# Issuing 88 small stores from ScalarE behind its own copies, in a block of attention, delta-net and feed-forward layer

## The chip, the core and the metric

The kernel runs on one core of a Trainium2 chip. The metric is the device time of one execution in microseconds (us). The engines of the core are named as in its profile: PE (matrix multiplication, with PEld for its weight loads), DVE (vector), ACT (scalar and activation functions, "ScalarE"), POOL (general) and SP (synchronisation; here it does nothing but issue DMAs). Each engine works through its own instruction stream in order; an instruction starts when the semaphores it waits for are set. A DMA is issued by an instruction in one engine's stream and then moves on its own.

## The reference

One transformer block for a sequence of 1024 positions of width 1024, in float32:

```
mod = silu(c) @ w_ada + b_ada                       # six modulation vectors
h   = rmsnorm(x) * (1 + sc1) + sh1
q_a,k_a,v_a, q_d,k_d,v_d,z_d, b_d,a_d = split(h @ w_in)
y_attn  = dilated_attention(q_a, k_a, v_a)          # 8 heads of 64, three dilated branches, bias
y_delta = gated_deltanet(q_d, k_d, v_d, z_d, b_d, a_d)
          # conv + silu, l2norm, chunked delta rule with a triangular solve per chunk
          # and a scan over the chunks, rmsnorm * silu(z)
x = x + g1 * (concat(y_attn, y_delta) @ w_out)
h = rmsnorm(x) * (1 + sc2) + sh2
x = x + g2 * ((silu(h @ w_gate) * (h @ w_up)) @ w_down)
return rmsnorm(x)
```

## The kernel before, in words

Every matrix product of full precision is made of three products of reduced-precision parts: an operand is split into a high part (a rounded copy, made by ACT at line 216) and a low part (the difference, made by POOL at line 217). `hh` and `hl` are the two parts of h, `wh_*` and `wl_*` those of a weight slab, `wr_*` the slab as it comes from memory (issued by SP at line 215).

The work runs in this order. First the modulation and the norm (to about 90 us) and the first projections; then the delta-net for head group 0 (convolutions, key products, the inverse of the triangular matrices on DVE, a scan over 8 blocks at about 268 to 312 us); the same for head group 1 (preparation at about 318 to 366 us, inverse at 373 to 402, scan at 441 to 476); the attention of 8 heads (from about 478 to 700 us); then the output projection and the feed-forward layer, which take the rest.

The delta-net and the attention are chains that go from engine to engine, and PE would stand still in them. So the remaining projections are laid into these waits as filling. A generator (`others()`, with the modulation's products mixed in by `mixed()`) hands out projection matmuls one small piece at a time in this order: z0, kd, qd, vd of group 1, z1, then for each of four head pairs the attention values va (two slabs) and the keys and queries a_4, a_0. A table `FILL` names a point of the chain (for instance `S0_0_0`, `trv3_0`, `sb0_6`) and the amount of filling to put ahead of it; `turn(name)` applies it, `ahead` draws the pieces, `hold` and `until` make sure that a projection is done before its reader needs it. Within these bounds the final order on each engine is decided by the scheduler of the framework, from dependencies, buffers, priorities (`urgent()` raises one) and its own model of durations. The issuing engine of a DMA is part of what that scheduler weighs.

A projection gathers in one of two PSUM banks ("g banks"). When it is done, an evacuating function copies it out of the bank on ACT:

- `va_evac(c)` (line 1056 on): copies 128x256 of attention values into a tile `va` (line 1061) and stores it into `va_d` (line 1062).
- `spill(name, dst)` (line 1065 on): copies a 128x512 bank in two halves into tiles `sp_*` (line 1070) and stores each (line 1071) into `pj_d` (delta-net: kd, qd, vd of group 1) or `qk_d` (attention keys and queries).
- `z_evac(g)` (line 611 on) does the same for z with a SiLU on ACT, a product on POOL and a store on SP; it is not touched.

The tiles `va` and `sp_*` share one tag `vt` with two buffers, so the third copy waits until the first store has landed.

In the delta scan (`delta_scan`), each of 8 steps has `state(n)`: PE products into a bank `st`, DVE makes R, PE multiplies by U (line 974), ACT copies VN out in two halves (line 978), PE multiplies VN into the new state (line 982), DVE adds it up. `readout(n-1)` makes the output o of the step before (ACT copy at line 1016), and `flip(n-3)` turns the output of three steps before by PE transposes (line 1038), copies it out on ACT (`yt`, line 1042, one buffer) and stores it in `yd_d` (line 1043).

Readers of the stored data: `fetch` (line 1151, xp from `pj_d`), `att_load` (lines 1209 and 1217, va and raw from `va_d` and `qk_d`; ACT then scales the raw queries to QS at line 1223 and rounds the raw keys to KS at line 1228, POOL makes the difference KL at line 1229, and the scores S of lines 1254 and 1255 use them), and the output projection, which reads `yd_d` at line 1355.

Before the change all 964 DMAs of the program are issued by SP, on one queue, in SP's order.

Of the kernel before, what the change touches and what calls it, by code (L numbers as in the profile page):

```python
# [23 lines left out]
HALF = 512  # L24
# [46 lines left out]
def build(tc, I, out):  # L71
    nc = tc.nc
# [20 lines left out]
    def urgent():  # L93
        return tc.high_priority(offset=6000)
# [42 lines left out]
    def sbank(name):  # L137
        return psb(name, "s", 2)
# [416 lines left out]
    @contextmanager  # L555
    def turn(name):

        with tc.issue_after(last[0].ins) if ahead(FILL.get(name, 0)) else ExitStack():
            yield
# [388 lines left out]
    def delta_scan(g, st):  # L948
# [84 lines left out]
        def flip(n, o):  # L1033
            tk = slice(n * P, (n + 1) * P)
            ps = sbank(f"yt{g}_{n}")
            with turn(f"sy{g}_{n}"):
                for q in range(2):
                    nc.tensor.transpose(
                        ps[:, q * P : (q + 1) * P], o[:, 2 * q : 2 * q + 2, :].rearrange("p h d -> p (h d)"), ident
                    )  # L1040
            yt = pd.tile([P, 2, P], F32, name=f"yt{g}_{n}", tag="yt", bufs=1)
            nc.scalar.copy(yt.rearrange("p q t -> p (q t)"), ps[:, 0:256])
            nc.sync.dma_start(_.yd[g][:, :, tk].rearrange("q p t -> p q t"), yt)

        kept, outs = {}, {}
        for n in range(8 + 3):
            if n < 8:
                state(n)
            if 1 <= n <= 8:
                outs[n - 1] = readout(n - 1, *kept.pop(n - 1))  # L1050
            if n >= 3:
                flip(n - 3, outs.pop(n - 3))
# [4 lines left out]
    def va_evac(c):  # L1057
        def f(tb, ps):
            t = pv.tile([P, 256], F32, name=f"va{c}_{tb}", tag="vt", bufs=2)
            with urgent():  # L1060
                nc.scalar.copy(t, ps[:, 0:256])
            nc.sync.dma_start(_.va[c][tb], t)
        return f

    def spill(name, dst):
        def f(hf, ps):
            for i in range(2):
                t = pv.tile([P, 256], F32, name=f"sp_{name}_{hf}_{i}", tag="vt", bufs=2)
                with urgent():
                    nc.scalar.copy(t, ps[:, 256 * i : 256 * i + 256])  # L1070
                nc.sync.dma_start(dst[:, HALF * hf + 256 * i : HALF * hf + 256 * i + 256], t)
        return f

    def va_end(c):
# [388 lines left out]
    for hf in range(2):  # L1463
# [4 lines left out]
        for d in range(KT):  # L1468
            slabs = [(wsplit(I["wo"][d, 0], 512, f"wo{d}_0_{hf}"), 0)]
            t = x2[d, hf]  # L1470
# [206 lines left out]
    for k in range(4):  # L1677
# [3 lines left out]
        t = px.tile([P, HALF], F32, name=f"t2_{k}", tag="m", bufs=5)  # L1681
# [232 lines left out]
```

## Time and profile before

| | |
|---|---|
| time, median of three runs | 1443.23 us (1440.9 to 1454.74) |
| profiled execution | 1445.04 us, its span 1443.3 us |
| mean granted PE clock | 0.985 |
| PE busy | 95% of the span |
| ACT, DVE, POOL busy | 46%, 61%, 21% |
| DMA queue, share of 16 engines | 54.4%, 244 MB |
| the moved stores | 88 of 128 KB each, between 177 and 610 us |

The span is the stretch from the first to the last instruction that the profiler recorded; the profiled execution's own time lies 1.7 us above it. Busy time of an engine leaves out what it spends waiting and issuing DMAs. A row of waits gives who waited (engine, tile, line), for whom, the total in us, how many times and the longest. A row of a timeline gives the start, the duration, the engine, the line, the operation and its tiles; in square brackets stands the idle time just before it and what ended it. "SPq" is SP issuing a DMA: its duration is that of the issue, not of the transfer.

### The profile page before, as it was taken

Reading aid. Unit: us, or ns where it says so; the run is one execution under the profiler, and the core shown is the slowest. Engines: PE = TensorE matmul, PEld = TensorE weight load, DVE = VectorE, ACT = ScalarE, POOL = GpSimd, SP = SyncE. Lnnn points to the kernel's source line nnn. Section 1 sums busy time; section 2 is a strip of 40 time slices with the busy share of each in tenths; the row PEclk is TensorE's granted clock in tenths of the full one; section 3 lists DMA queues with packets and bytes.
Section 4 is the critical chain, followed back from the end, with each engine's and each line's share of the span. In section 5 each row is a group of like instructions: output and inputs, shape, how many; then the busy total and the mean of one; then the engine's idle time right before and its main releaser. Section 6 shows DMA issues by size and latency. Waiting matters only on the chain.

```text
span 1443.3 us, 24528 instructions
## 1 busy us (share of the span) xinstructions
PE 1372.5 (95%) x8984; PEld 1112.9 (77%) x8984; DVE 875.8 (61%) x1660; ACT 668.3 (46%) x1283; POOL 310.3 (21%) x279
## 2 busy tenths in 40 slices
PE   7998989997999699999998989999999999999997
PEld 4776857787879677777876868888888888888885
DVE  3587762665746223376426997757576776474487
ACT  3487523348233345576337743333333333444456
POOL 1345412243333334454244300000000000000000
PEclk9998999999999999999999999999999999999999
DMA  8736464466541643651375445636354565766666
GB/s 300 244 119 172 139 197 148 148 183 185 156 121 45 190 109 103 187 147 67 127 229 163 147 137 177 204 108 211 124 182 144 163 217 183 265 213 202 194 222 234
DMA packets 171921, 245.69 MB, mean 170 GB/s; under 512 B 33078, under 2 KB 76391, under 8 KB 171800
## 3 DMA queue, kind: packets, MB, share of 16 engines
q1 hardware_dynamic: 171800, 244.12, 54.4%
q8 instruction: 71, 1.16, 0.4%
q14 instruction: 50, 0.41, 0.1%
HBM read 181.30 MB, written 67.48 MB: 172 GB/s over the span
## 4 chain that ended last, share of the span: by engine, by line
PE 58%; DVE 6%; DMA 4%; ACT 2%; issue 1%; POOL 1%; SPq 0%; DVEq 0%; ACTq 0%; POOLq 0%
PE wua L1536 8%; PE wga L1536 8%; PE X L1731 6%; PE g_a L570 5%; PE wuc L1536 4%; PE Z L1731 4%; PE wgc L1536 4%; PE wo L570 3%; PE y L1295 2%; PE Y L1731 2%; PE tr L1278 2%; PE wgb L1536 2%; PE wub L1536 2%; PE g_va L593 2%; PE S L1254 1%
## 5 line engine op out<-in xcount | busy, mean ns | idle before, releaser
L1526 DVE TENSOR_TENSOR wl_db<-wr_db,wh_db 128x512 fp32r<-128x512 f32 x77 | 53.2, 691 | 76.4 <-ACT wh_db L1525 76.2
L1525 ACT CAST wh_db<-wr_db 128x512 fp32r<-128x512 f32 x77 | 47.9, 622 | 98.7 <-PE X L1731 41.3
L1258 DVE CUSTOM_DVE_ANT_0 X<-S,ng 128x512 f32<-128x512 f32 (+3 forms) x64 | 36.7, 587 | 71.5 <-PE S L1255 58.4
L1263 ACT ACTIVATE X<-X,sc 128x128 f32<-128x128 f32 (+7 forms) x64 | 49.4, 773 | 42.0 <-DVE sc L1258 36.6
L1731 PE MATMUL X<-wl_db,wh_da 128*128 128x512 f32 x176 | 68.6, 390 | 0.2 <-DVE wl_db L1526 0.2
L1731 PE MATMUL X<-wh_db,wh_da 128*128 128x512 f32 x176 | 68.6, 390 | 0.0
L1731 PE MATMUL X<-wh_db,wl_da 128*128 128x512 f32 x176 | 68.5, 389 | 0.0
L1265 POOL TENSOR_SCALAR X<-X,sc 128x128 f32<-128x128 f32 (+7 forms) x64 | 49.9, 782 | 82.3 <-DVE sc L1264 80.8
L1526 DVE TENSOR_TENSOR wl_da<-wr_da,wh_da 128x512 fp32r<-128x512 f32 x77 | 52.7, 686 | 1.2 <-ACT wh_da L1525 1.2
L570 PE MATMUL g_a<-hh,wh_a 128*128 128x512 f32 x128 | 53.2, 416 | 0.0
L570 PE MATMUL wo<-yh,wh_wo 128*128 128x512 f32 x128 | 51.5, 404 | 1.0 <-DVE xo L1346 1.0
L570 PE MATMUL wo<-yl,wh_wo 128*128 128x512 f32 x128 | 50.5, 394 | 0.9 <-DVE yl L1357 0.9
L570 PE MATMUL g_a<-hl,wh_a 128*128 128x512 f32 x128 | 51.0, 398 | 0.0
L570 PE MATMUL g_a<-hh,wl_a 128*128 128x512 f32 x128 | 50.7, 396 | 0.0
L570 PE MATMUL wo<-yh,wl_wo 128*128 128x512 f32 x128 | 50.6, 396 | 0.0
L1525 ACT CAST wh_da<-wr_da 128x512 fp32r<-128x512 f32 x77 | 47.3, 616 | 5.8 <-PE wua L1536 5.8
L1525 ACT CAST wh_wg_s<-wg_s 128x512 fp32r<-128x512 f32 x33 | 20.5, 622 | 55.4 <-PE wuc L1536 23.5
L1278 PE MATMUL tr<-ident,X 128*128 128x128 f32 x288 | 43.3, 277 | 2.8 <-DVE et L1281 1.8
L1254 PE MATMUL S<-KS,QS 128*128 128x512 f32 (+3 forms) x96 | 35.7, 380 | 10.2 <-ACT KS L1228 8.0
L217 POOL TENSOR_TENSOR wl_wo<-wr_wo,wh_wo 128x512 fp32r<-128x512 f32 x24 | 33.1, 1382 | 56.9 <-ACT wh_wo L216 55.9
L1295 PE MATMUL y<-et,va 128*64 128x128 f32 x576 | 42.8, 279 | 0.0
L1278 PEld LDWEIGHTS tr<-ident,X 128*128 128x128 f32 x288 | 33.0, 140 | 11.9 <-issue 4.6
(545 smaller groups left out, 4366.5 us busy)
## 6 DMA issues: line engine op xcount, KB each, us to landing
wr_da<-ao_d SPq DMA_DIRECT2D x77, 256.0 KB, 3.3
wm<-in_wada SPq DMA_DIRECT2D x64, 256.0 KB, 3.7
wr_wu<-in_wu SPq DMA_DIRECT2D x50, 256.0 KB, 2.9
wr_wg<-in_wg SPq DMA_DIRECT2D x48, 256.0 KB, 3.0
ao_d<-a SPq DMA_DIRECT2D x44, 256.0 KB, 2.7
wr_wd<-in_wdn SPq DMA_DIRECT2D x44, 256.0 KB, 3.1
wr_db<-wt_d SPq DMA_DIRECT2D x44, 256.0 KB, 3.0
ao_d<-as SPq DMA_DIRECT2D x33, 256.0 KB, 2.0
```

Source lines behind the costliest of these rows:

```text
L217: (eng or nc.gpsimd).tensor_tensor(out=lo[:, :n], in0=raw[:, :n], in1=hi[:, :n].bitcast(F32), op=ALU.subtract)
L570: last[0] = nc.tensor.matmul(ps, a[:, w0], b[k0 + k4][:, cs], start=(i == 0), stop=(i == n - 1))
L1254: nc.tensor.matmul(ps[:, 0 : c1 - c0], QS[:, qs], KS[:, c0:c1], start=True, stop=False)
L1258: nc.vector.tensor_tensor_reduce(out=X[:, c0:c1], in0=ps[:, 0 : c1 - c0], in1=ng[:, u + c0 : u + c1], scale=1.0, scalar=(3e38 if m is None ...
L1263: nc.scalar.activation(X[:, 0:nk], X[:, 0:nk], AF.Exp, scale=-1.0, bias=m, accum_out=sc[:, 2:3])
L1265: nc.gpsimd.tensor_scalar(out=X[:, 0:nk], in0=X[:, 0:nk], scalar1=sc[:, 3:4], scalar2=0.0, op0=ALU.mult, op1=ALU.add)
L1278: nc.tensor.transpose(ps[:, (kb - c0) * P : (kb - c0 + 1) * P], X[:, kb * P : kb * P + P], ident)
L1295: nc.tensor.matmul(yps[64 * e : 64 * e + 64, yc], va[:, kb, 64 * e : 64 * e + 64], ets[e][:, kb, :], start=(kb == 0), stop=(kb == qb),)
L1525: nc.scalar.copy(hi, src)
L1526: (eng or nc.vector).tensor_tensor(out=lo, in0=src, in1=hi.bitcast(F32), op=ALU.subtract)
L1536: nc.tensor.matmul(ps, a[:, w0], b, start=(first and k == 0 and n_ == 0), stop=(k == 3 and n_ == 2), skip_group_check=True,)
L1731: nc.tensor.matmul(bank[b], a[:, ts_], w, start=(first and f == 0 and n_ == 0), stop=(f == NF - 1 and n_ == 2), skip_group_check=True,)
```

## The change

Three kinds of stores are issued by ACT, right behind the ACT copy that fills their tile, and no longer by SP: 16 turned delta outputs (yt to `yd_d`), 16 tiles of attention values (va to `va_d`), 56 halves of spilled projections (24 to `pj_d`, 32 to `qk_d`). Nothing else in the source is changed. The order in which the scheduler lays out the instructions of all engines follows from it.

```
         nc.scalar.copy(yt.rearrange("p q t -> p (q t)"), ps[:, 0:256])
-        nc.sync.dma_start(_.yd[g][:, :, tk].rearrange("q p t -> p q t"), yt)
+        nc.scalar.dma_start(_.yd[g][:, :, tk].rearrange("q p t -> p q t"), yt)
...
             with urgent():
                 nc.scalar.copy(t, ps[:, 0:256])
-            nc.sync.dma_start(_.va[c][tb], t)
+            nc.scalar.dma_start(_.va[c][tb], t)
...
                 with urgent():
                     nc.scalar.copy(t, ps[:, 256 * i : 256 * i + 256])
-                nc.sync.dma_start(dst[:, HALF * hf + 256 * i : HALF * hf + 256 * i + 256], t)
+                nc.scalar.dma_start(dst[:, HALF * hf + 256 * i : HALF * hf + 256 * i + 256], t)
```

In the built program SP's stream goes from 923 instructions to 836 and ACT's from 1147 to 1236: the 88 stores, and one more load of a function table, since ACT's functions come in another order (27 loads, where there were 26). PE's instructions are the same ones; between about 268 and 366 us, around 494 to 510 us and a little between 640 and 700 us some filling matmuls stand earlier or later than before relative to the chains.

More of the change, by code (lines that the diff above doesn't have):

```diff
@@ L1042, in flip @@
             nc.scalar.copy(yt.rearrange("p q t -> p (q t)"), ps[:, 0:256])
-            nc.sync.dma_start(_.yd[g][:, :, tk].rearrange("q p t -> p q t"), yt)
+            nc.scalar.dma_start(_.yd[g][:, :, tk].rearrange("q p t -> p q t"), yt)
         kept, outs = {}, {}
@@ L1061, in f @@
                 nc.scalar.copy(t, ps[:, 0:256])
-            nc.sync.dma_start(_.va[c][tb], t)
+            nc.scalar.dma_start(_.va[c][tb], t)
         return f
@@ L1070, in f @@
                     nc.scalar.copy(t, ps[:, 256 * i : 256 * i + 256])
-                nc.sync.dma_start(dst[:, HALF * hf + 256 * i : HALF * hf + 256 * i + 256], t)
+                nc.scalar.dma_start(dst[:, HALF * hf + 256 * i : HALF * hf + 256 * i + 256], t)
         return f
```

## The prediction

> **What bounds the kernel now.** I read the page first, then busy time by stretches, then the waits of TensorE (PE), then the waits of the queue's own engine SP, then the rows of the moved stores.
>
> ```profile
> span 1443.3 us, 24528 instructions
> PE 1372.5 (95%) x8984; PEld 1112.9 (77%) x8984; DVE 875.8 (61%) x1660; ACT 668.3 (46%) x1283; POOL 310.3 (21%) x279
> q1 hardware_dynamic: 171800, 244.12, 54.4%
> ```
>
> PE is the bound: 1372.5 of 1443.3 us. A change that adds no PE work can win only PE's idle time, 70.8 us in all, and can lose only by making more of it. The one DMA queue is busy for 54.4% of the span, so bandwidth is not what binds.
>
> Busy time in nine stretches that together cover 180 to 700 us; four of them are shown with the sum. The moved stores lie between 177 us and 610 us:
>
> ```profile
> core 0: us, PE busy (x) PEld busy (x) DVE busy (x) ACT busy (x) POOL busy (x), PEclk, DMA share, GB/s
> ...
> 318.00:366.00 48.00, 40.35 (x383) 35.35 (x381) 32.76 (x45) 38.42 (x70) 20.90 (x15) 0.93 0.65 186
> ...
> 441.00:477.00 36.00, 35.67 (x294) 34.33 (x294) 23.76 (x86) 10.66 (x33) 14.18 (x16) 1.00 0.21 64
> 477.00:505.00 28.00, 17.04 (x113) 15.21 (x112) 3.69 (x5) 10.08 (x16) 11.07 (x7) 0.88 0.73 216
> ...
> 612.00:700.00 88.00, 83.61 (x702) 65.04 (x700) 61.03 (x183) 60.71 (x130) 40.00 (x41) 1.00 0.37 107
> sum 520.00, PE 487.42 PEld 394.78 DVE 271.39 ACT 239.25 POOL 183.85; mean PE 54.16 PEld 43.86 DVE 30.16 ACT 26.58 POOL 20.43
> ```
>
> PE is idle for 520.00 − 487.42 = 32.6 us there. The start of attention (477 to 505) holds 28.00 − 17.04 = 11.0 us of it, the delta preparation of head group 1 (318 to 366) 7.7 us; the second delta scan (441 to 477) only 0.3 us. Who ends these gaps, from the waits of PE between 160 and 700 us (total, times, longest):
>
> ```profile
> PE S L1254 <- ACT KS L1228: 8.0, 1, 8.0
> ...
> PE S L1255 <- POOL KL L1229: 3.0, 2, 1.6
> PE kk_k L779 <- DVE qk L785: 3.0, 2, 2.6
> PE trq_0False L717 <- ACT cv L537: 2.3, 1, 2.3
> ...
> PE ps_bp L760 <- DVE nbp L754: 1.8, 1, 1.8
> ```
>
> No row of that view names one of the 88 stores, or a copy that feeds one. So what SP gains by being rid of them does not reach PE by itself.
>
> **What the change removes from SP.** The stores' rows (issue in ns, minimum, median, maximum) and SP's longest waits for their copies (total, times, longest):
>
> ```profile
> L1071 SPq DMA_DIRECT2D qk_d<-sp_a x32: 319/380/2456, 405.8 to 607.0; - x32
> L1071 SPq DMA_DIRECT2D pj_d<-sp_kd x8: 319/402/1145, 178.3 to 210.1; - x8
> L1071 SPq DMA_DIRECT2D pj_d<-sp_qd x8: 320/382/1838, 214.4 to 234.5; - x8
> L1071 SPq DMA_DIRECT2D pj_d<-sp_vd x8: 326/406/1402, 239.8 to 319.4; - x8
> L1062 SPq DMA_DIRECT2D va_d<-va x16: 319/346/1217, 372.8 to 502.8; - x16
> L1043 SPq DMA_DIRECT2D yd_d<-yt x16: 360/371/427, 276.2 to 476.9; - x16
> ```
>
> ```profile
> SPq L1071 <- ACT sp_a L1070: 37.5, 15, 7.1
> ...
> SPq L1062 <- ACT va L1061: 16.9, 8, 6.6
> ...
> SPq L1043 <- ACT yt L1042: 11.0, 12, 1.6
> ```
>
> These three waits are 65.4 us of SP's time. SP then issues the loads behind them earlier, as far as their buffers are free. I value that at 0: the loads that PE waits for are not behind these stores in any row above. The lower bound is the gaps below, which it may help to close.
>
> **What it adds to ScalarE (ACT).** The issues, by the medians: 32 × 0.380 + 8 × 0.402 + 8 × 0.382 + 8 × 0.406 + 16 × 0.346 + 16 × 0.371 = 33.2 us, on an engine that is busy for 239.25 of the 520 us. No DMA in this trace is issued by ACT, so its price there is bounded by SP's rows: 0.32 us from below, the largest maximum, 2.46 us, from above; I take SP's medians, since the access patterns are the same. The store has to wait for its own copy, and everything behind it on ACT waits too. What ACT regains are the copies that wait for a landing because the store was issued late, of which the largest row is small:
>
> ```profile
> ACT sp_a L1070 <- DMA qk_d<-sp_a: 6.1, 3, 2.9
> ```
>
> Spills and attention values beside the projections (177 to 268 and 366 to 441 us, and 505 to 610 us): PE runs from double-buffered banks there and none of its waits names the spill copies. I cost 56 + 16 issues there at +1.0 us: nearly all are hidden behind PE's matmuls; without that cover the 27.2 us of these issues would be paid. Bounds 0 to +6, the upper being what three 2 us hold-ups of the kind in the row of maxima would cost.
>
> **The delta scans.** The scan's chain goes through ACT twice a step. Here is ACT in one step of the first scan:
>
> ```profile
> 280.15 0.37 ACT L1042 COPY yt<-yt 128x256 f32<-128x256 f32 x1 [1.10 <-PE yt L1038]
> 280.74 0.27 ACT L978 COPY VN<-st 128x128 f32<-128x128 f32 x1 [0.22 <-PE st L974]
> 281.42 0.27 ACT L978 COPY VN<-st 128x128 f32<-128x128 f32 x1 [0.41 <-PE st L974]
> ```
>
> In the built order of the changed kernel (which instruction stands behind which on each engine; it holds no times) the store of yt stands either between the yt copy and the first VN, or between the two VN copies. In the first place it issues from 280.52 to about 280.89, and VN starts 0.15 us late; behind that VN wait PE's L982 and then the new state. In the second place it takes 0.37 of 0.41 us that were free. With 16 steps I take 16 × 0.15 = +2.4, rounded to +2.5 us: PE has about one projection matmul in hand at each of these places, which does not cover all. Bounds: 0, and twice the issue (0.74 us, so VN 0.52 late) in all 16 steps, +8.3.
>
> [...]
>
> **The preparation of group 1 (318 to 366).** ACT is the tightest here, 38.42 of 48 us. The built order puts four stores there (4 × 0.38 = 1.5 us) and pulls SiLUs of z in between exponentials, which makes nine function-table loads up to the last exponential, where there were six. A load's price:
>
> ```profile
> L750 ACT ACT_TABLE_LOAD x2 | 2.6, 1283 | 0.0
> ```
>
> So three more are 3.8 us, and the chain kk, trq, trv comes about 5.4 us later. Against it PE has more to do meanwhile: the built order has 2 to 6.3 us of projection matmuls of z earlier, 6.3 at trv. At trv PE would then be 5.4 us late with 6.3 us of work done ahead, so 0.9 us are won, if the next stage lets them be. That stage, the inverse, has this much room (SP issuing the load of the inverse tn, its landing as the median of that DMA, and PE's first use):
>
> ```profile
> 405.32 0.37 SPq L874 DMA_DIRECT2D tn<-tn_d  x1
> ...
> tn<-tn_d SPq DMA_DIRECT2D x1, 512.0 KB, 4.4
> ...
> 413.88 0.79 PE L897 MATMUL lv<-tn,dt 32*32 32x32 f32 x38
> ```
>
> It lands at 409.7, 4.2 us before PE needs it, so at most 4.2 us of any gain here survive, and a chain that starts 5.4 us late would eat the room and more. I take −1.0 us, bounds −4.2 and +5.4.
>
> **The start of attention (477 to 505).** The chain of waits in this window:
>
> ```profile
> 480.00 5.17 PE g_va L593 x43
> ...
> 492.16 1.25 POOL wl_a L217
> ...
> 493.43 0.33 SPq L215
> ...
> 494.94 6.09 DMA raw<-qk_d
> ...
> 501.06 1.05 ACT KS L1228
> ...
> 502.18 2.35 POOL KL L1229
> ...
> 504.57 0.79 PE S L1255 x2
> ```
>
> PE has issued the scores of the first head and stands from 494 to 502 for KS of the second, whose raw data lands at 501.03. That chain stays: SP's loads around it stand in the same order. But PE's order differs: between the scores of the first head and of the second the built program now has 35 matmuls of 128×512 of the projection a (none before), and 3 more ahead of the KL scores. The first row gives 5.17/43 = 0.12 us for a 256-wide one; a 512-wide one at twice that is 0.24, so 35 fill 8.4 us: the 8.0 us wait, almost exactly. On ACT two spill stores now stand ahead of this KS; they wait for PE's bank at about 500 and put KS at 501.3, 0.2 late. Later, between these scores and the fourth block's, the order has that fill no more, and the transposes there will wait about 1 us for the exponentials. I take −8.0 − 0.7 (the three matmuls) + 0.2 + 1.0 = −7.5 us; bounds −11.0 (all idle time of the stretch) and 0.
>
> **Sum.** −7.5 − 1.0 + 2.5 + 1.0 = −5.0 us. The profiled execution took 1445.04 us, 1.7 more than its span; so 1440.0. Its time is 0.1% over the median of the three runs, 1443.23 us, which is nothing beside their spread (1440.9 to 1454.74).
>
> **Rivals.** One per cent, 14.4 us, is about what a measurement of this kernel can tell from no change.
>
> A. *An issue on ACT is far dearer than on SP, and the scan pays it.* Place: the 16 yt stores and the preparation. Price: at 1.2 us an issue (the maxima of sp_kd, sp_vd and va are 1.1 to 1.4) VN starts 1.2 − 0.22 = 1.0 us late in 16 steps, +16; the four stores of the preparation cost 4.8 with the tables' 3.8, less the 4.2 of room, +4.4; of the 32 sp_a issues a third falls where attention's exponentials are waited for, +12; the attention's gain is halved, −4. Together +28, 1473. It decides from about 0.8 us an issue. For it: the long maxima, and the scan's small free spaces. Against it: the medians lie close to the minima, and yt's own maximum is 0.43 us. [...]
>
> B. *The attention's gain is given back.* The work put into the 8 us gap is missing between 612 and 700 us, where PE idles 88.00 − 83.61 = 4.4 us already, and the attention's own chain sets the end of the stretch. Then −7.5 falls to about 0, and the rest of the sum leaves +2.5: 1447.5. For it: the built order has up to 3.7 us less fill before some products y there. Against it: the fill stands level again long before, at the fourth block.
>
> C. *Both gaps close and ACT's issues are hidden.* −11.0 from attention's start, −4.2 from the preparation, 0 from scans, and 2 of the remaining 13.9 us of idle time between 180 and 700 us by loads that SP issues earlier: −17, 1428. For it: 65 us of SP's waits go. Against it: the raw data's landing, which ends the large gap, is not among what moves.
>
> **How the numbers follow.** Forecast (1440) 0.34; A 0.28; B 0.12; C 0.26. Faster by over 1% (under 1430.6) is C and a little of the forecast: 0.27. Slower by over 1% (over 1459.5) is A, with a part of B: 0.31. Within 1%: 0.42. The likeliest case's own range comes from its bounds taken halfway: 1431 to 1450. The range for 8 in 10 takes in most of C and the lower half of A: 1424 to 1468.
>
> **What would show it.** In the profile after: the wait of S for KS falls from 8.0 to under 1 us, and PE's idle time in that stretch by 7 to 9 us; the issues appear on ACT at 0.32 to 0.45 us median; VN's starts follow yt's stores within 0.2 us and the scans' length from first to last yt grows by 1 to 2 us each; PE's idle time in the preparation stays at 5 to 9 us. The forecast is wrong if the issues on ACT are over 0.8 us, if the scan's steps grow by over 0.5 us, if tn lands after PE gets to lv, or if the KS wait stays since KS itself has moved later with the fill.

## The result

The change makes the kernel slower: 1460.22 us median against 1447.61 us for the kernel before on the same chips, a ratio of 1.0095 with a 95% interval of 1.0072 to 1.0117. The forecast was 1440.0 and the range 1424 to 1468. The comparisons leave out executions that are more than 1.5% over the fastest of their kernel; that drops one of this kernel's ten (2674.55 us), one of the ten of `before_z24` and four of the twelve of `yt_only` below, whose loss its ratio therefore understates.

The profiled execution took 1464.23 us, 4.0 over the median. Its page, in the lines that answer to those shown of before:

```profile
span 1462.5 us, 24493 instructions
PE 1397.9 (96%) x8984; PEld 1132.9 (77%) x8984; DVE 879.4 (60%) x1660; ACT 668.9 (46%) x1284; POOL 309.4 (21%) x279
...
PEclk9998999999975999999999999999999999999999
...
q1 hardware_dynamic: 157080, 232.58, 50.7%
q10 hardware_dynamic: 14720, 11.54, 2.4%
```

PE executes the same 8984 matmuls but is busy for 25.4 us longer (1397.9 against 1372.5). It did not wait more (its idle time went from 70.8 to 64.6 us), it ran slower: the row of the granted clock has a 7 and a 5 in slices 12 and 13 of 40, about 402 to 475 us. The stores are the new queue q10; in the traces SP issues 964 DMAs before and 876 after, ACT none and 88. Busy time by the same stretches (span, then PE, PEld, DVE, ACT, POOL busy, then the granted clock):

```profile
318.00:366.00 48.00, 44.80 (x385) 39.25 (x384) 27.27 (x40) 36.40 (x67) 17.61 (x11) 0.92 0.58 170
...
414.00:441.00 27.00, 22.78 (x276) 17.50 (x274) 7.97 (x21) 7.14 (x18) 3.00 (x5) 0.64 0.34 89
441.00:477.00 36.00, 36.00 (x318) 32.10 (x319) 12.35 (x36) 7.62 (x20) 5.39 (x7) 0.56 0.07 23
477.00:505.00 28.00, 27.48 (x226) 26.36 (x226) 18.60 (x64) 8.49 (x27) 10.65 (x13) 1.00 0.24 69
```

From 441 to 477 us PE is busy for all 36.00 us, as before (35.67), but at 0.56 of its clock, where it had 1.00. Who ends PE's waits between 160 and 720 us, and the place itself on PE's timeline:

```profile
PE lv L897 <- DMA tn<-tn_d: 4.2, 1, 4.2
PE S L1255 <- POOL KL L1229: 3.0, 2, 1.8
...
PE kk_q L779 <- DMA qd<-cv_d: 2.1, 1, 2.1
```

```profile
418.32 0.39 PE L570 MATMUL g_a<-hh,wl_a 128*128 128x512 f32 x1
422.93 1.92 PE L897 MATMUL lv<-tn,dt 32*32 32x32 f32 x64 [4.22 <-DMA tn<-tn_d]
```

The 8.0 us wait of S for KS is gone, as forecast. In its stead lv, the first product of the inverse of group 1, waits 4.2 us for its input tn, which was there 4.2 us early before. Windows of 4 us around it show what the wait does (PE busy, matmuls, granted clock, share of DMA, GB/s):

```profile
416.00:420.00 4.00, 2.71 (x12) 1.00 0.60 205
420.00:424.00 4.00, 1.07 (x40) 0.68 1.06 188
424.00:428.00 4.00, 4.00 (x85) 0.50 0.21 72
...
468.00:472.00 4.00, 4.00 (x21) 0.50 0.02 4
472.00:476.00 4.00, 4.00 (x35) 0.92 0.00 0
```

The clock falls to 0.50 during the wait and stays there for 50 us. Following the same instruction through both traces gives the account (start in us, before and after):

| instruction | before | after | shift |
|---|---|---|---|
| yt copy of step 6, first scan (ACT) | 307.15 | 308.31 | +1.2 |
| third va copy (ACT) | 378.80 | 383.52 | +4.7 |
| first VN, second scan (ACT) | 439.04 | 465.74 | +26.7 |
| yt copy of step 6, second scan (ACT) | 473.95 | 503.82 | +29.9 |
| KS of the second head (ACT) | 501.06 | 533.49 | +32.4 |
| KS of the third head (ACT) | 538.93 | 559.25 | +20.3 |
| KS of the last head (ACT) | 650.81 | 670.95 | +20.1 |

So, in this execution, 4.7 us are lost by the end of the preparation, then 4.2 in the wait, some 20 at half clock (of the 25.2 from +4.7 to +29.9, less 4.2 and less what the scan added), 2.5 up to the attention, and 12.1 are won back at its start, where PE has the filling to do. The rest of the program, untouched, adds nothing.

The new order alone does not make the 4.7 us. Three runs below (`after_keep`, `after_z48`, `after_rewarm`) have the same instructions in the same order on every engine up to lv, and there the third va copy starts at 378.00, 378.21 and 382.62 us. Where the copy is late, the clock had dipped before it: between 318 and 366 us it is 0.92 here and 0.93 in `after_rewarm`, but 1.00 in `after_keep`. What the four traces have in common is that tn is late as measured against PE's own progress: its load is issued 13.4, 8.9, 9.3 and 12.5 us later than before, in the order of this kernel and the three, which is 8.6 to 9.9 us more than the shift of that va copy. The room was 4.2 us.

Where tn falls behind can be followed on SP. Here are the issues on SP in the trace after (the first qd load of that group came at 333.04):

```profile
343.49 0.35 SPq L1094 DMA_DIRECT2D wm<-in_wada  x1
343.94 0.37 SPq L1179 DMA_DIRECT2D qd<-cv_d  x1
...
380.70 0.32 SPq L849 DMA_DIRECT2D nt<-lt_d  x1
...
418.68 0.38 SPq L874 DMA_DIRECT2D tn<-tn_d  x1
```

Before, the second qd load was issued at 333.13 and nt at 368.33. Now a load of modulation weights (wm) stands ahead of this qd load. It waits for a buffer that PE's modulation products have to free, and SP, which works in order, holds the qd load behind it: SP's waits between 318 and 382 us are led by this row.

```profile
SPq L1094 <- PE mods L197: 13.3, 5, 6.8
```

The longest of these waits, 6.8 us, is the one ahead of the second qd load (4.4 us in `after_keep`).

### The profile page after: what moved, and what is told of

It is laid out like the page before. It is cut to its first block, busy times and chain, and to the rows that moved or that the text cites. A ratio compares the mean times of both kernels' runs of the same rounds, so it can differ in the third digit from the quotient of the medians.

```text
span 1462.5 us, 24493 instructions
## 1 busy us (share of the span) xinstructions
PE 1397.9 (96%) x8984; PEld 1132.9 (77%) x8984; DVE 879.4 (60%) x1660; ACT 668.9 (46%) x1284; POOL 309.4 (21%) x279
## 4 chain that ended last, share of the span: by engine, by line
PE 73%; DVE 12%; DMA 7%; ACT 3%; issue 3%; POOL 1%; SPq 1%; DVEq 0%; ACTq 0%; POOLq 0%
PE wua L1536 8%; PE wga L1536 7%; PE X L1731 6%; PE g_a L570 5%; PE wuc L1536 4%; PE Z L1731 4%; PE wgc L1536 4%; PE wo L570 2%; PE y L1295 2%; PE Y L1731 2%; PE tr L1278 2%; PE f L237 2%; PE g_va L593 2%; DVE tm L865 2%; PE wgb L1536 2%
## 5 line engine op out<-in xcount | busy, mean ns | idle before, releaser
L197 PE MATMUL mods<-wm,cc 128*32 128x128 f32 x512 | 33.0, 295 | 9.9 <-DMA wm<-in_wada 5.4
```

The source lines that it names most:

```text
L197: nc.tensor.matmul(ps[32 * j : 32 * j + 32, 0 : 32 * nt], win, v[:, j], start=False, stop=last, skip_group_check=True)
```

## The experiments

Times of different sessions are set against the full change's 1460.22 us below; the kernel before, measured in each, had medians of 1446.9 to 1449.5 us there.

The theory after reading the traces, called T: the issues on ACT cost next to nothing; the change makes the scheduler lay out the preparation of group 1 in another order, in which nt and so tn come late (13 us in the trace above); PE runs into the wait, the clock falls, and the half clock is the loss. The rival R: the issues on ACT themselves cost the time.

**One part of the change at a time.** Each edit leaves one of the three lines on ACT and returns the other two to SP.

```
va_only:  line 1062 nc.scalar.dma_start; lines 1043 and 1071 nc.sync.dma_start
sp_only:  line 1071 nc.scalar.dma_start; lines 1043 and 1062 nc.sync.dma_start
yt_only:  line 1043 nc.scalar.dma_start; lines 1062 and 1071 nc.sync.dma_start
```

> Only the 16 stores of attention values are issued by ACT. In the built order everything up to the attention is as before, and between the first and the second head's scores stand the 35 projection matmuls that close the gap there. Theory T (the change loses through the order of the preparation of group 1, a late tn and the half clock that follows it, and wins at the start of attention): no wait of lv for tn, clock at about 0.985 or above, the 8.0 us wait for KS gone, time 10 to 13 us under before (about 1435). Theory R (the issues on ACT themselves cost time, wherever they stand): no gain, 0 to +6 us.

Measured: 1437.83 us, 0.9931 (0.9906 to 0.9956) of the kernel before. The stretches of its profiled execution in which the full change lost and won:

```profile
414.00:441.00 27.00, 26.98 (x519) 22.09 (x518) 11.84 (x26) 10.81 (x27) 5.65 (x6) 1.00 0.21 61
...
477.00:505.00 28.00, 25.35 (x146) 21.96 (x146) 3.96 (x5) 11.46 (x21) 10.90 (x8) 0.94 0.65 189
```

PE's idle time at the start of attention falls from 11.0 us to 2.7 and the clock holds. T is borne out: 16 issues on ACT, and the time goes down. This version beats both kernels.

> Only the 56 stores of spilled projections are issued by ACT. The built order has the preparation of group 1 changed much as in the full change, and the start of attention as before. Theory T: the load of nt is 8 to 13 us later than before, lv waits 2 to 6 us for tn, the granted clock falls to 0.5 for some 50 us, and the 8.0 us wait for KS stays; time 20 to 32 us over before. [...] Theory R: 56 issues of 0.33 us, a part of them exposed, +3 to +15 us with the clock unchanged.

Measured: 1465.0 us, 1.0105 (1.0068 to 1.0143). The waits of PE, and three windows of 4 us:

```profile
PE S L1254 <- ACT KS L1228: 7.6, 1, 7.6
...
PE lv L897 <- DMA tn<-tn_d: 3.6, 1, 3.6
```

```profile
420.00:424.00 4.00, 4.00 (x55) 0.50 0.19 66
...
444.00:448.00 4.00, 4.00 (x27) 0.50 0.38 111
448.00:452.00 4.00, 4.00 (x74) 0.81 0.02 4
```

The late tn and the half clock come with the spills alone, 30 us long in the profiled execution, which is the fastest of the four. The ratio is that of the full change; T had expected 20 to 32 us over before and it is 15. That the clock came back earlier than in the full change fits this, but was seen in that one execution only.

> Only the 16 stores of turned delta outputs are issued by ACT. Theory T: the scans grow by 1 to 2 us each at most; the order of the preparation changes little and has fewer table loads, so tn is not late, the clock stays, the wait for KS stays: -3 to +4 us against before. Theory R: the scans hold the exposed issues, so +5 to +10 us here, the largest cost per store of the three parts.

Measured: a median of 1463.95 us over executions from 1443.22 to 1475.32, ratio of those that the comparison keeps 1.0039 (1.0002 to 1.0076). The expectation of T missed: the clock falls here too, in some executions and not in others (the mean clock goes from 0.961 to 0.983). In the profiled one PE has two gaps close together:

```profile
PE g_a L570 <- ACT sp_a L1070: 1.9, 1, 1.9
...
PE lv L897 <- DMA tn<-tn_d: 1.6, 1, 1.6
```

Together 3.5 us, and the clock was at 0.50 from 420 to 448 us. The scan itself grew little: from the first to the seventh yt copy the second scan takes 27.3 us, before 26.9. The second qd load is not late here (335.22 us, 2.1 after before), and still nt's product starts at 381.45, 9.3 later: the last lt store ahead of it on SP is issued at 372.22, behind more wm loads, and SP waits 15.2 us for PE's modulation products between 318 and 382 us. So a held-up qd load is not the only way to a late tn.

**Is it the clock?** First, more work ahead of lv; then work that nobody needs, in the place of the wait; then the same behind the wait.

```
after_z48:     LEVELS = ("qd", 4), ("z1", 48)            # 36 in the full change
after_keep:    before lv of group 1:
               for i in range(22):
                   nc.tensor.matmul(ps, hh[0][:, 0:P], hh[1][:, 0:HALF], ...)
after_rewarm:  12 of the same matmuls, right behind the first products of lv
```

> The full change, with 48 instead of 36 us of projection work held ahead of the first product of the inverse (lv) of group 1. PE then reaches lv 12 us later, after tn has landed. Theory T: no wait for tn, the clock stays at 1.0 there, and the 25 us of wait and half clock go: 22 to 27 us under the full change (about 1435 to 1440), less what the attention misses of that work later. Theory R: the late tn is a symptom and the clock is lost elsewhere or not what costs; the time stays within 8 us of the full change.

Measured: 1447.72 us, 1.0005 (0.9979 to 1.0031) of before, 12.5 us under the full change. The clock was 1.00 in all windows from 366 to 505 us. The direction is that of T, the size is half: a part of the 12 us of projection work that went ahead was missed later, with 5.6 us of waits of yt for DVE in the scans, where the full change has 2.0. The rest of the difference was not followed.

> The full change, with 22 matmuls of 128x512 whose result nobody reads put on PE between the last projection matmul and the first product of the inverse (lv) of group 1: 22 x 0.23 = 5.0 us of extra work in the place of the 4.2 us wait for tn. Everything else, the late tn too, stands as in the full change. Theory T (the half clock after the wait is what costs): the clock stays at 1.0 from 414 to 505 us, and the time is 16 to 22 us under the full change, about 1440, though PE does more work. Theory R (the clock falls for another reason, or PE's late arrival itself costs): the clock falls all the same, time within 5 us of the full change.

Measured: 1443.52 us, 0.9975 (0.9951 to 0.9998) of before and 16.7 us under the full change. In the first rows the useless work and the wait that is left; in the others the clock:

```profile
413.04 5.15 PE L1147 MATMUL keep<-hh,hh 128*128 128x512 f32 x22
418.47 1.20 PE L897 MATMUL lv<-tn,dt 32*32 32x32 f32 x64 [0.28 <-DMA tn<-tn_d]
```

```profile
414.00:441.00 27.00, 26.05 (x489) 20.64 (x488) 12.44 (x27) 11.65 (x29) 5.65 (x6) 1.00 0.29 73
441.00:477.00 36.00, 35.24 (x295) 33.45 (x294) 23.73 (x83) 10.31 (x32) 10.68 (x14) 1.00 0.18 52
```

This is the plainest of the runs: all 88 stores are on ACT; SP, DVE and POOL run the order of the full change to the end; tn comes 5.4 us after PE's last projection product (5.15 of them now filled), where the full change has 4.2; PE does 22 matmuls more; and the time is that of the kernel before or a little under. What costs in the full change is that PE stood still there. Of the 24.7 us between the two profiled spans 5.5 lie ahead of the wait already (third va copy at 378.00 against 383.52), so the medians' 16.7 are the better measure.

> The full change with 12 matmuls of 128x512 whose result nobody reads, put right behind the first 16 products of lv in group 1, so behind the 4.2 us wait for tn and not in its place. The wait and the fall of the clock stay. Theory T2 (the clock returns after a dense stretch of 128-row matmuls, and in the full change it stays down since the small products of the inverse keep such a stretch from coming): it is back at 1.0 within 10 us of lv, and the time is 8 to 16 us under the full change, though 12 x 0.43 = 5.1 us of work at half clock are added. Theory R2 (once down, the clock stays down for 30 to 50 us whatever follows): 2 to 6 us over the full change.

Measured: 1450.3 us, 1.0028 (1.0006 to 1.0049) of before, 9.9 us under the full change. The wait, the added work, and the windows:

```profile
422.15 1.06 PE L898 MATMUL lv<-tn,dt 32*32 32x32 f32 x32 [4.33 <-DMA tn<-tn_d]
423.14 4.94 PE L903 MATMUL warm<-hh,hh 128*128 128x512 f32 x12
```

```profile
420.00:424.00 4.00, 1.85 (x34) 0.56 0.66 146
424.00:428.00 4.00, 4.00 (x11) 0.59 0.19 66
428.00:432.00 4.00, 4.00 (x107) 1.00 0.01 4
```

With the same wait the clock is back after 5 us of dense matmuls, not after 50. So in this pair the length of the fall is set by what follows it. In the inverse PE alternates products of 32x32 and 64x64 with three or four wide ones, and in the full change this does not bring the clock back until the scan is well under way (0.50 up to 472 us).

**A wait without the change.** The same fall should come in the kernel before, if PE is sent to lv too early.

```
before_z24:   LEVELS = ("qd", 4), ("z1", 24)             # 36 in the kernel before
```

> The kernel before, all stores issued by SP, with 24 instead of 36 us of projection work held ahead of lv of group 1. PE reaches lv about 12 us earlier, at 402, and tn lands at 410 as before: a wait of 6 to 8 us without any issue on ACT. Theory T: the granted clock falls to 0.5 for 30 to 50 us there, time 12 to 25 us over before. Theory R: the wait alone, +0 to +8 us, since the work left out is done later.

Measured: 1449.04 us, 1.0014 (0.9979 to 1.0049): no loss, and the expectation of T missed. The wait did come, shorter than expected, and the clock fell, but for one window:

```profile
PE lv L897 <- DMA tn<-tn_d: 3.1, 1, 3.1
```

```profile
404.00:408.00 4.00, 0.93 (x58) 1.00 1.13 207
408.00:412.00 4.00, 4.00 (x74) 0.62 0.24 85
412.00:416.00 4.00, 4.00 (x36) 0.95 0.41 98
```

Behind lv stand seven wide matmuls in a row here, three in the full change; that agrees with `after_rewarm`, but the wait was shorter too. Two of its ten executions, at 1464 and 1467 us, have a mean clock of 0.969 and 0.968, under all of the kernel before (0.973 to 0.988), so a longer fall probably happens here too; they were not profiled. Whether a wait of 3 to 4 us makes a long fall is thus not settled by its length alone.

**Why is tn late?** The loads wm at plain priority in the full change, the same in the kernel before as a control, the qd loads at raised priority in the full change, and wm at plain priority with the va stores alone.

```
after_wmplain, before_wmplain, va_wmplain:
-                with urgent():
-                    nc.sync.dma_start(w, I["wada"][...])
+                nc.sync.dma_start(w, I["wada"][...])
after_qdfirst:
-                nc.sync.dma_start(t, _.cv[j])
+                with urgent():
+                    nc.sync.dma_start(t, _.cv[j])
```

> The full change, with the loads of the modulation's weights (wm) given no raised priority. In the built order no wm load stands ahead of the second qd load, the three extra table loads of ACT are two fewer, and the load of nt stands right behind the last lt store. Theory T: nt 6 to 10 us earlier than in the full change, no wait of lv for tn above 2 us, clock not under 0.9 from 414 to 477 us; time 15 to 25 us under the full change, about 1437. Theory R (the 88 issues on ACT are the cost): within 6 us of the full change.

> Control: the kernel before with the wm loads given no raised priority. Theory T: tn is not late before, so there is little to win: -5 to +4 us against before. If it wins 10 us or more, the priority of wm is a gain of its own, and the run of the full change without it does not speak for theory T.

Measured: 1438.16 us and 0.9946 (0.9919 to 0.9972) for the full change with this edit, 22 us under the full change; 1449.21 us and 1.0012 (0.9989 to 1.0034) for the control. In the first, nt is issued at

```profile
365.26 0.33 SPq L849 DMA_DIRECT2D nt<-lt_d  x1
```

15.4 us earlier than in the full change, and lv waits for nothing. With tn in time, all 88 stores on ACT are a gain of 0.5%, and the edit alone is none. So the raised priority of wm is part of what makes tn late, though the edit gives the other instructions a new order as well.

> The full change, with the loads of the convolved rows (qd, L1179 there) at raised priority. In the built order ACT has fewer table loads up to the last exponential than in the kernel before, but a wm load still stands ahead of the second qd load on SP. It tells apart which of the two makes nt late. If it is the wm load that waits for PE's modulation products (theory S): the second qd load is issued after 340 us, nt's product on DVE starts after 379, lv waits for tn, clock under 0.8 from 414 to 441, time within 8 us of the full change. If it is ACT's table loads (theory A): nt starts before 375, no wait for tn, time 15 us or more under the full change.

Measured: 1459.24 us, 1.0076 (1.0047 to 1.0105). ACT's extra table loads ahead of the last exponential are gone, but the second qd load (on SP's timeline) is hardly earlier, and lv waits (PE's waits):

```profile
341.28 0.33 SPq L1180 DMA_DIRECT2D qd<-cv_d  x1
```

```profile
PE lv L897 <- DMA tn<-tn_d: 4.0, 1, 4.0
```

The product of nt starts at 380.2 us, before 372.2, in the full change 385.0. The 4.8 us between cannot be put down to the table loads, since with all of them `after_keep` and `after_z48` have nt at 379.4. What S foretold came, but not by its mechanism alone: no wm load waits long ahead of the second qd load here; SP waits 6.2 us, in two places, for the rows to land before it may load them. How nt's lateness divides between SP's queue, the rows' landing, ACT and PE's filling stays open.

> Only the stores of attention values on ACT, and the wm loads at plain priority. Both edits alone left the wait for tn away; theory T expects no more than va_only gives, 8 to 14 us under before, since the two do not add up: the one closes the gap at the start of attention, the other does nothing for a tn that is not late.

Measured: 1446.81 us, 0.9988 (0.9967 to 1.0009), a miss: 9 us more than `va_only`. Here PE's modulation products wait 12.2 us in nine places for their own weights; in `after_wmplain` it is 4.7 us. That the raised priority has its use while SP still issues the spills would fit this; the kernel before lost nothing by the same edit, with 9.2 us of these waits.

## Why the prediction was wrong

The measured time lies inside the stated range, but on the side that the range left to rival A, whose dear issues are in no trace; that it is inside is luck, and the direction was wrong.

**Attention's start, the largest term, was right in kind and too small.** Forecast −7.5, measured −12.1 between the KS of the second and third heads. I subtracted 1.0 for transposes that would wait, and left out that in the trace before the matmuls behind the 8 us wait had run at a lower clock: 0.50 from 500 to 506 us, 0.88 over the stretch. How the 4.6 us more divide between these was not tested.

**The issues on ACT cost what SP's medians said, or less.** Here are three of the rows after:

```profile
L1071 ACTq DMA_DIRECT2D qk_d<-sp_a x32: 326/327/503, 407.6 to 626.0; - x32
L1062 ACTq DMA_DIRECT2D va_d<-va x16: 326/332/346, 374.7 to 518.0; - x16
L1043 ACTq DMA_DIRECT2D yd_d<-yt x16: 366/367/509, 278.4 to 509.0; - x16
```

The medians are 0.33 to 0.37 us, and the longest of these 0.51, where SP had 2.46 (one of the sp_kd stores took 1.15, as on SP). Rival A needed 0.8. Twice the issue in every step, the upper bound, would have cost the scans 8.3 us; from first to seventh yt copy the first took 30.4 us, before 31.3, and the second grew by 0.4 (`yt_only`) to 0.7 us. My own +2.5 for the scans was too high.

**The preparation is the step that failed.** I forecast −1.0 with bounds of −4.2 and +5.4. Two things are wrong in it. The size: I took the chain to be 5.4 us late, from table loads and issues on ACT, with PE as late and so little of it felt. In the four traces of this order nt was 7.2 to 12.9 us late and tn 8.6 to 9.9 us late against PE, twice the room of 4.2. A part of that, at most the 4.4 to 6.8 us of that wait, is SP holding a qd load behind a wm load; the rest stays open. The prediction followed SP's order around the attention, and not around the qd loads in the middle of the preparation. And the price: I named "tn lands after PE gets to lv" as a sign of error, but priced it as waiting only. A wait of 4.2 us cost about 20 more in the profiled execution, because the clock fell and stayed down through the stage after it; filling the wait gave back 16.7 us of the median (`after_keep`). The trace of before held a hint: the clock of 0.88 in the one stretch with an 8 us wait, which I quoted and did not use.

The time without the clock's part was near the forecast. The mean over executions of time times mean clock is 1417.2 us after and 1421.3 before (over its executions in the later sessions), 4.1 us less, where the sum said 5.0 less; the mean clock is 0.971 after and 0.982 before. This product is only a rough measure, since not all time hangs on PE's clock, but `after_z48`, `after_keep` and `after_wmplain`, in whose traces the clock holds there, are 2 to 9 us under before.

None of the rivals was it. B (given back later) fails, since the shift stays at 20 us to the end. Of C's two gains the larger, the gap at the start of attention, did come; the other did not.

## What to carry to other kernels

Price a wait on PE by what the clock does behind it, not by its length: here a gap of 4.2 us ahead of a stage of small products cost about five times as much, and 22 wide matmuls in its place or 12 right behind it, some 5 us of useless work, gave back 16.7 and 9.9 us. When an edit moves only the issuer of a DMA, read the whole new order of the queue that it left as well as that of the engine that it joins; here a load that moved up on SP was part of the loss. Before a shift of some us is put down to an order, look at a second execution of the same order: here they differ by 5 us. If a change has several parts that a scheduler weighs together, try them one by one: of these three, only the stores of attention values are a gain as they are.

## What the runs showed of the hardware

The fall of PE's clock, with its numbers: 0.50 after waits of 3.6 us (`sp_only`) and 4.2 us (the full change), and after two of 1.9 and 1.6 us close together (`yt_only`); for 28 to 50 us where small products followed, and, after a wait of 4.33 us, for under 8 us where 12 wide matmuls did (`after_rewarm`: 0.56 and 0.59 in two windows of 4 us, 1.00 in the next). The length of a wait does not order these: `before_z24` has a short fall after 3.1 us (0.62 and 0.95 in two windows of 4 us) and `yt_only` a long one after 1.9 and 1.6. In the full change PE, busy from 423 us on with small products between a few wide ones, stayed at 0.50 up to 472 us; that it is the small products which keep the clock down rests on the one test of `after_rewarm`.

An issue on ACT can run beside ACT's compute. In the trace after:

```profile
282.19 0.27 ACT L978 COPY VN<-st 128x128 f32<-128x128 f32 x1
282.25 0.38 ACTq L1043 DMA_DIRECT2D yd_d<-yt  x1
```

The store is issued while the VN copy ahead of it in the stream is still at work, so a part of its 0.38 us is hidden even on the engine itself. By the starts and durations in that trace this holds for 42 of the 88 stores, and for 10.8 of their 33.0 us.
